# A Winograd-style 3x3 convolution: the first image pair by another queue, row sums between the loads, whole images in one store

## The chip, the core and the metric

The kernel runs on one core of a Trainium2 chip. A core has a matrix engine (TensorE, in profiles PE, with its weight loads shown apart as PEld), a vector engine (DVE), a scalar engine (ACT), GpSimd (POOL) and a sync engine (SP), all started together and ordered against each other by semaphores alone. Operands lie in SBUF with 128 partitions; TensorE writes its sums to PSUM, here eight banks of 128 x 512 fp32. Sixteen DMA engines move data between HBM and SBUF. SP issues transfers that hardware turns into packets (queue q1 in the profile); GpSimd issues transfers that software turns into packets (queue q0), and in this kernel those convert fp32 to fp16 on the way.

The metric is the device time of one launch in microseconds (us), as the median of several runs.

## What is computed

```python
x: (16, 64, 64, 64) fp32; weight: (128, 64, 3, 3) fp32
x_pad = np.pad(x, ((0, 0), (0, 0), (1, 1), (1, 1)))
for b, co, ci, kh, kw:
    output[b, co] += weight[co, ci, kh, kw] * x_pad[b, ci, kh:kh+h, kw:kw+w]
```

It is a 3x3 convolution with zero padding, over 16 images of 64 channels and 64 x 64 points, into 128 channels. The input has 16.78 MB, the weights 0.29 MB, the output 33.55 MB.

## The kernel before, in words

**Tiling.** Two images of 64 channels fill the 128 partitions, so the input comes as eight pairs, each a tile `xs` of 128 x 64 x 64 in fp16. A matmul uses 64 partitions, so the two images of a pair (`b2` = 0 and 1) run on the two halves of the array. Output rows come in four blocks of 16 rows per pair (`blk`), that is 8 even rows and 8 odd rows for each image.

**Fewer matmuls by row sums.** For each pair the kernel also forms `ss`, the sums of neighbouring input rows 2j and 2j+1. A block needs three accumulation groups (`group`, lines 110 to 145): `U` applies the middle row of weights, G1, to `ss` (6 matmuls); `A` applies G21 = w2 - w1 and G0 = w0 to rows of `xs` (12 matmuls) and gives, with `U` added, the even rows; `Bt` applies G01 = w0 - w1 and G2 = w2 (12 matmuls) and gives, with `U` added, the odd rows. A block so has 30 matmuls, and the kernel 960. Scalar copies `U` from PSUM to `ut` (line 151); Vector adds `A` and `ut` (line 156) and `Bt` and `ut` (line 159) into the output tile `ot`; SP stores each block of each image with one DMA of 512 KB (line 160), 64 in all. There are 16 such tiles.

**Weights.** SP loads them as they lie, one row of 576 fp32 per output channel (line 41). Scalar and Vector cast and reorder them into `w16`, each tap twice side by side (lines 57 to 68); TensorE transposes them by nine matmuls with an identity (lines 79 to 84), which gives each tap on both halves of the partitions; lines 86 to 90 copy and subtract them from PSUM into `Wt`.

**Loads and sums.** GpSimd issues all loads of `x`, with conversion to fp16 (line 48): pair 0 in four pieces, every other pair in two of 32 rows, 18 DMAs in all. For pair 0 Vector forms `ss` in four pieces; for pairs 1 to 7 GpSimd does so in two pieces of 2 x 1024 elements a partition (line 100). The loop of lines 44 to 53 issues all loads first, and the sums stand in line 94's loop behind it. Each engine works through its own instructions in order. `tc.keep_in_program_order` fixes the place of an instruction among those of its engine; without it a planner places the instructions by program order and due times. Waits, on data as on a free buffer, are put in by the framework.

Of the kernel before, what the change touches and what calls it, by code (L numbers as in the profile page):

```python
# [8 lines left out]
F32 = mybir.dt.float32  # L9
F16 = mybir.dt.float16  # L10


@with_exitstack
def kernel(
    ctx: ExitStack,
    tc: tile.TileContext,
    x: bass.AP,
    weight: bass.AP,
    out: bass.AP,
):  # L20
    nc = tc.nc
    B, CI, H, W = x.shape
    CO = weight.shape[0]
    assert H == 64 and W == 64 and CI == 64 and CO == 128 and B % 2 == 0
    NP = B // 2
    RB = 8

    x_rows = x.rearrange("b c h w -> (b c) h w")
    out_rows = out.rearrange("b co h w -> b co h w")
    w_flat = weight.rearrange("co ci kh kw -> co (ci kh kw)")  # L30

    const = ctx.enter_context(tc.tile_pool(name="const", bufs=1))
    psum = ctx.enter_context(tc.tile_pool(name="psum", bufs=8, space=bass.MemoryType.PSUM))
    xpool = ctx.enter_context(tc.tile_pool(name="xpool", bufs=1))
    opool = ctx.enter_context(tc.tile_pool(name="opool", bufs=16))
    spool = ctx.enter_context(tc.tile_pool(name="spool", bufs=3))
    upool = ctx.enter_context(tc.tile_pool(name="upool", bufs=4))


    w_raw = const.tile([CO, CI, 9], F32)  # L40
    nc.sync.dma_start(w_raw.rearrange("p c t -> p (c t)"), w_flat)
    xs = []
    ident = const.tile([128, 128], F16)
    for p in range(NP):
        xt = xpool.tile([128, H, W], F16, tag=f"xs{p}", name="xs")
        cuts = [0, 18, 32, 48, 64] if p == 0 else [0, 32, 64]
        for lo, hi in zip(cuts[:-1], cuts[1:]):
            nc.gpsimd.dma_start(  # L48
                xt[:, lo:hi, :], x_rows[128 * p : 128 * p + 128, lo:hi, :]
            )  # L50
            if p == 0 and lo == 0:
                make_identity(nc, ident)
        xs.append(xt)


    w16 = const.tile([CO, 9, 2, CI], F16)
    for kh in range(3):
        src = (
            w_raw[:, :, 3 * kh : 3 * kh + 3]
            .rearrange("p c t -> p t c")  # L60
            .unsqueeze(2)
            .to_broadcast([CO, 3, 2, CI])
        )
        dst = w16[:, 3 * kh : 3 * kh + 3, :, :]
        if kh == 1:
            nc.vector.tensor_copy(dst, src)  # L66
        else:
            nc.scalar.copy(dst, src)  # L68

    Wt = const.tile([128, 5, 3, CO], F16)  # L70
    G0, G21, G1, G01, G2 = range(5)

    def wrow(i):
        return Wt[:, i, :, :].rearrange("p t c -> p (t c)")

    wps = {}
    for kh in (1, 0, 2):
        wp = psum.tile([128, 512], F32, tag="acc", name="wp")
        for k in range(3):
            nc.tensor.matmul(  # L80
                wp[:, k * CO : k * CO + CO],
                w16[:, 3 * kh + k, :, :].rearrange("p d c -> p (d c)"),
                ident,
            )
        wps[kh] = wp[:, 0 : 3 * CO]
    nc.vector.tensor_copy(wrow(G1), wps[1])  # L86
    nc.scalar.copy(wrow(G0), wps[0])  # L87
    nc.vector.tensor_sub(wrow(G21), wps[2], wrow(G1))  # L88
    nc.vector.tensor_sub(wrow(G01), wps[0], wrow(G1))  # L89
    nc.scalar.copy(wrow(G2), wps[2])  # L90


    ss = []
    for p in range(NP):
        st = spool.tile([128, H // 2, W], F16, tag="ss", name="ss")
        v = xs[p].rearrange("p (j i) c -> p j i c", i=2)
        step = 8 if p == 0 else 16
        for lo in range(0, H // 2, step):
            eng = nc.vector if p == 0 else nc.gpsimd
            add = eng.tensor_add(  # L100
                st[:, lo : lo + step, :], v[:, lo : lo + step, 0, :], v[:, lo : lo + step, 1, :]
            )
            if p > 0:
                tc.keep_in_program_order(add)
        ss.append(st)

        for blk in range(4):
            j0 = blk * RB

            def group(wi_rows):  # L110

                tiles = [
                    psum.tile([128, RB, W], F32, tag="acc", name="acc") for _ in range(2)
                ]
                n = 3 * len(wi_rows)
                i = 0
                for wi, off in wi_rows:
                    for kw in (1, 0, 2):
                        c_lo, c_hi = max(0, 1 - kw), min(W, W + 1 - kw)
                        for b2 in range(2):  # L120
                            p0 = 64 * b2
                            lo, hi = j0, j0 + RB
                            if off is None:
                                rhs = ss[p][p0 : p0 + 64, lo:hi, c_lo + kw - 1 : c_hi + kw - 1]
                            else:
                                while 2 * lo + off < 0:
                                    lo += 1
                                while 2 * (hi - 1) + off > H - 1:
                                    hi -= 1
                                first = 2 * lo + off  # L130
                                last = 2 * (hi - 1) + off
                                rhs = xs[p][
                                    p0 : p0 + 64,
                                    first : last + 1 : 2,
                                    c_lo + kw - 1 : c_hi + kw - 1,
                                ]
                            nc.tensor.matmul(  # L137
                                tiles[b2][:, lo - j0 : hi - j0, c_lo:c_hi],
                                Wt[p0 : p0 + 64, wi, kw, :],
                                rhs,  # L140
                                start=i == 0,
                                stop=i == n - 1,
                            )
                        i += 1
                return tiles

            U = group([(G1, None)])
            us = []
            for b2 in range(2):
                ut = upool.tile([128, RB, W], F32, tag="ut", name="ut")  # L150
                nc.scalar.copy(ut, U[b2])  # L151
                us.append(ut)
            ots = [opool.tile([128, RB, 2, W], F32, tag="ot", name="ot") for _ in range(2)]
            A = group([(G21, 1), (G0, -1)])
            for b2 in range(2):
                nc.vector.tensor_add(ots[b2][:, :, 0, :], A[b2], us[b2])  # L156
            Bt = group([(G01, 0), (G2, 2)])
            for b2 in range(2):
                nc.vector.tensor_add(ots[b2][:, :, 1, :], Bt[b2], us[b2])  # L159
                nc.sync.dma_start(  # L160
                    out_rows[2 * p + b2, :, blk * 16 : blk * 16 + 16, :],
                    ots[b2].rearrange("p j i c -> p (j i) c"),
                )


# [28 lines left out]
```

## Time and profile before

| | |
|---|---|
| median of 8 runs | 133.12 us (132.27 to 134.37) |
| the profiled execution | 133.49 us |
| its span on the core | 131.7 us |
| PE busy | 108.9 us, 83% of the span |
| DVE busy | 84.5 us, 64% |
| POOL busy | 39.6 us, 30% |
| ACT busy | 38.2 us, 29% |
| HBM read and written | 17.07 MB and 33.55 MB |
| store queue q1 | 9360 packets, 33.85 MB |
| load queue q0 | 2592 packets, 8.39 MB (counted as fp16) |

The span is what the engines and queues cover on the core; the execution's own time is 1.8 us longer. A busy share is an average over the whole span, so it doesn't say which engine is waited for at a given moment. The page also draws the span as 40 slices of 3.3 us; each digit is the busy share in tenths, and PEclk is the clock that TensorE was granted:

```profile
PE   0408999700999999999999999999999999999910
...
POOL 6823111117999283009201910290000000000000
PEclk9999999985569999999999999999999999999998
DMA  4899999999999999999999999999999999888884
GB/s 102 112 178 215 214 215 276 275 276 276 277 279 272 285 272 279 276 328 412 419 418 419 413 417 421 418 417 416 418 418 412 421 391 372 348 342 336 330 331 178
```

TensorE has a hole in the ninth and tenth slice (26 to 33 us). The DMA row is nearly full to the end. The last row counts a converting load at its fp16 size.

### The profile page before, as it was taken

The page shows a single profiled execution, that of the slowest core. Times are in us where ns is not written, and L with a number is a line of the kernel's source. Part 1 is how long each engine was busy: PE and PEld are TensorE (multiplying, and loading weights), DVE is VectorE, ACT ScalarE, POOL GpSimd, SP SyncE. Part 2 cuts the span into 40 slices and gives each one's busy share as a digit, 9 for nine tenths or more (in the row PEclk, how much of TensorE's full clock was granted, in tenths as well). Part 3 has the DMA queues.
Part 4 walks back from the last instruction along what each step waited for, and adds up shares of the span by engine and source line. Part 5 has one row for each costly group of instructions (what it writes and reads, how often), then busy time and mean ns, then how long its engine had stood idle before and what let it go on. Part 6 is the DMA issues. An engine that isn't in the chain of part 4 may idle for free.

```text
span 131.7 us, 2482 instructions
## 1 busy us (share of the span) xinstructions
PE 108.9 (83%) x969; PEld 54.1 (41%) x969; DVE 84.5 (64%) x136; ACT 38.2 (29%) x69; POOL 39.6 (30%) x38
## 2 busy tenths in 40 slices
PE   0408999700999999999999999999999999999910
PEld 0203444200345555555555555555555555555500
DVE  0226577710047778777877777777777777877750
ACT  3604033300303333333333333333333333333300
POOL 6823111117999283009201910290000000000000
PEclk9999999985569999999999999999999999999998
DMA  4899999999999999999999999999999999888884
GB/s 102 112 178 215 214 215 276 275 276 276 277 279 272 285 272 279 276 328 412 419 418 419 413 417 421 418 417 416 418 418 412 421 391 372 348 342 336 330 331 178
DMA packets 11963, 42.39 MB, mean 322 GB/s; under 512 B 1328, under 2 KB 1456, under 8 KB 11952
## 3 DMA queue, kind: packets, MB, share of 16 engines
q1 hardware_dynamic: 9360, 33.85, 64.4%
q0 software_dynamic: 2592, 8.39, 33.0%
q8 instruction: 7, 0.11, 0.3%
q14 instruction: 4, 0.03, 0.1%
HBM read 17.07 MB, written 33.55 MB: 384 GB/s over the span
## 4 chain that ended last, share of the span: by engine, by line
PE 67%; DMA 21%; issue 4%; POOL 2%; DVE 1%; ACTq 1%; DVEq 0%; ACT 0%; POOLq 0%
PE acc L137 67%; DMA xs<-in_x_dram 21%; POOL ss L100 2%; ACTq L189 1%; DVE ot L156 1%; POOL xs L48 0%; DVEq L189 0%; DVE ot L159 0%; POOL ident masks.py:197 0%; ACT ut L151 0%; POOLq L178 0%
## 5 line engine op out<-in xcount | busy, mean ns | idle before, releaser
L137 PE MATMUL acc<-xs,Wt 64*128 64x504 f16 (+3 forms) x768 | 90.9, 384 | 0.0
L137 PEld LDWEIGHTS <-Wt 64*128 64x128 f16 x960 | 53.3, 97 | 66.4 <-issue 13.5
L156 DVE TENSOR_TENSOR ot<-acc,ut 128x512 f32<-128x512 f32 x64 | 41.2, 686 | 33.0 <-PE acc L137 16.6
L151 ACT COPY ut<-acc 128x512 f32<-128x512 f32 x64 | 34.4, 589 | 78.5 <-issue 74.6
L159 DVE TENSOR_TENSOR ot<-acc,ut 128x512 f32<-128x512 f32 x64 | 41.2, 685 | 1.0 <-PE acc L137 1.0
L100 POOL TENSOR_TENSOR ss<-xs 128x1024 f16<-128x1024 f16 x14 | 29.3, 2125 | 28.7 <-issue 28.7
L137 PE MATMUL acc<-ss,Wt 64*128 64x504 f16 (+1 forms) x192 | 27.6, 392 | 12.3 <-POOL ss L100 7.8
L48 POOL DMA_DIRECT2D xs<-in_x_dram x18 | 9.7, 548 | 20.4 <-DMA xs<-in_x_dram 19.6
L80 PE MATMUL wp<-ident,w 128*128 128x128 f16 x9 | 1.3, 307 | 4.4 <-DVE w L66 4.4
L100 DVE TENSOR_TENSOR ss<-xs 128x512 f16<-128x512 f16 x4 | 1.7, 422 | 4.8 <-DMA xs<-in_x_dram 4.8
L66 DVE CAST w<-w_raw 128x384 f16<-128x384 f32 x1 | 0.8, 834 | 3.5 <-DMA w_raw<-in_weight_dram 3.5
L80 PEld LDWEIGHTS <-w 128*128 128x128 f16 x9 | 0.8, 133 | 4.7 <-DVE w L66 4.4
L68 ACT CAST w<-w_raw 128x384 f16<-128x384 f32 x2 | 1.7, 876 | 1.5 <-DMA w_raw<-in_weight_dram 1.5
L90 ACT CAST Wt<-wp 128x384 f16<-128x384 f32 x1 | 0.5, 478 | 5.1 <-DVE Wt L88 5.1
L68 ACT ACT_TABLE_LOAD x1 | 1.3, 1283 | 0.7 <-PEq L178 0.7
L88 DVE TENSOR_TENSOR Wt<-wp,Wt 128x384 f16<-128x384 f32 x1 | 0.6, 558 | 0.1
L86 DVE CAST Wt<-wp 128x384 f16<-128x384 f32 x1 | 0.5, 549 | 0.0
L89 DVE TENSOR_TENSOR Wt<-wp,Wt 128x384 f16<-128x384 f32 x1 | 0.5, 548 | 0.0
L87 ACT CAST Wt<-wp 128x384 f16<-128x384 f32 x1 | 0.5, 478 | 0.1
masks.py:199 POOL TENSOR_SCALAR_AFFINE_SELECT ident<-ident 128x128 f16<-128x128 f16 x1 | 0.3, 307 | 0.1
masks.py:197 POOL MEMSET ident<- 128x128 f16 x1 | 0.2, 224 | 0.0
L178 POOL MEMSET const-float32-0.0<- 128x1 f32 x1 | 0.1, 100 | 0.2 <-issue 0.2
(3 smaller groups left out, 0.3 us busy)
## 6 DMA issues: line engine op xcount, KB each, us to landing
out_dram<-ot SPq DMA_DIRECT2D x64, 512.0 KB, 9.9
xs<-in_x_dram POOLq DMA_DIRECT2D x14, 512.0 KB, 24.3
xs<-in_x_dram POOLq DMA_DIRECT2D x2, 256.0 KB, 8.1
w_raw<-in_weight_dram SPq DMA_DIRECT2D x1, 288.0 KB, 2.8
xs<-in_x_dram POOLq DMA_DIRECT2D x1, 288.0 KB, 7.0
xs<-in_x_dram POOLq DMA_DIRECT2D x1, 224.0 KB, 7.2
```

Source lines behind the costliest of these rows:

```text
L48: nc.gpsimd.dma_start(xt[:, lo:hi, :], x_rows[128 * p : 128 * p + 128, lo:hi, :])
L66: nc.vector.tensor_copy(dst, src)
L68: nc.scalar.copy(dst, src)
L80: nc.tensor.matmul(wp[:, k * CO : k * CO + CO], w16[:, 3 * kh + k, :, :].rearrange("p d c -> p (d c)"), ident,)
L86: nc.vector.tensor_copy(wrow(G1), wps[1])
L88: nc.vector.tensor_sub(wrow(G21), wps[2], wrow(G1))
L100: add = eng.tensor_add(st[:, lo : lo + step, :], v[:, lo : lo + step, 0, :], v[:, lo : lo + step, 1, :])
L137: nc.tensor.matmul(tiles[b2][:, lo - j0 : hi - j0, c_lo:c_hi], Wt[p0 : p0 + 64, wi, kw, :], rhs, start=i == 0, stop=i == n - 1,)
L151: nc.scalar.copy(ut, U[b2])
L156: nc.vector.tensor_add(ots[b2][:, :, 0, :], A[b2], us[b2])
L159: nc.vector.tensor_add(ots[b2][:, :, 1, :], Bt[b2], us[b2])
L189: with _tile.TileContext(nc) as tc:
```

## The change

The change has three parts.

*Pair 0 and the weights.* Pair 0 is no longer loaded by GpSimd with conversion. SP loads it as fp32 into `x0`, which takes one slot of the output tiles, in four pieces right behind the weights. Scalar casts the pieces into `xs[0]`, and Vector forms pair 0's row sums from the fp32 tile. The weights are cast by one GpSimd instruction without reordering; TensorE then reads every ninth element of `w16` and needs two matmuls of 64 columns for each tap, one for each half of the partitions. The first copy, of G1, moves from Vector to Scalar, and the order of the following work on Scalar and Vector is fixed.

*Loads and sums.* Every other pair is loaded by one DMA. GpSimd's order becomes: weight cast, loads of pairs 1 to 4, sums of pair 1, sums of pair 2, load 5, sums of pair 3, load 6, sums of pair 4, load 7, and then the sums of pairs 5, 6 and 7. The `xs` tiles have five slots in place of eight.

*Stores.* `ot` holds a whole image, 16 KB per partition, in eight slots. Each image is stored by one DMA after its last block; only the last pair's images are stored in two halves.

```diff
-    xpool = ctx.enter_context(tc.tile_pool(name="xpool", bufs=1))
-    opool = ctx.enter_context(tc.tile_pool(name="opool", bufs=16))
+    xpool = ctx.enter_context(tc.tile_pool(name="xpool", bufs=5))
+    opool = ctx.enter_context(tc.tile_pool(name="opool", bufs=8))
...
+    w_raw = const.tile([CO, CI * 9], F32)
+    nc.sync.dma_start(w_raw, w_flat)
+    x0 = opool.tile([128, H, W], F32, tag="ot", name="x0")
+    cuts = [(0, 18), (18, 34), (34, 50), (50, 64)]
+    for lo, hi in cuts:
+        nc.sync.dma_start(x0[:, lo:hi, :], x_rows[0:128, lo:hi, :])
     ident = const.tile([128, 128], F16)
...
+    make_identity(nc, ident)
+    w16 = const.tile([CO, CI * 9], F16)
+    keep(nc.gpsimd.tensor_copy(w16, w_raw))
+
+    xs = {0: xpool.tile([128, H, W], F16, tag="xs", name="xs")}
+
+    def load(p):
+        xs[p] = xpool.tile([128, H, W], F16, tag="xs", name="xs")
+        keep(nc.gpsimd.dma_start(xs[p], x_rows[128 * p : 128 * p + 128, :, :]))
+
+    for p in range(1, 5):
+        load(p)
...
+    def sums(eng, p, src, lo, n):
+        if p not in ss:
+            ss[p] = spool.tile([128, H // 2, W], F16, tag="ss", name="ss")
+        v = src.rearrange("p (j i) c -> p j i c", i=2)
+        keep(
+            eng.tensor_add(
+                ss[p][:, lo : lo + n, :], v[:, lo : lo + n, 0, :], v[:, lo : lo + n, 1, :]
+            )
         )
...
-    for kh in (1, 0, 2):
+    for kh in (1, 2, 0):
         wp = psum.tile([128, 512], F32, tag="acc", name="wp")
         for k in range(3):
...
+            t = 3 * kh + k
+            for q in (0, 64):
+                nc.tensor.matmul(wp[q : q + 64, k * CO : k * CO + CO], w16[:, t::9], ident)
         wps[kh] = wp[:, 0 : 3 * CO]
...
+    keep(nc.scalar.copy(wrow(G1), wps[1]))
+    sums(nc.vector, 0, x0, 0, RB)
+    keep(nc.vector.tensor_sub(wrow(G21), wps[2], wrow(G1)))
+    keep(nc.vector.tensor_sub(wrow(G01), wps[0], wrow(G1)))
+    for n, (lo, hi) in enumerate(cuts):
+        keep(nc.scalar.copy(xs[0][:, lo:hi, :], x0[:, lo:hi, :]))
+        if n == 0:
+            keep(nc.scalar.copy(wrow(G0), wps[0]))
+            keep(nc.scalar.copy(wrow(G2), wps[2]))
+        if n < 3:
+            sums(nc.vector, 0, x0, RB * (n + 1), RB)
...
     for p in range(NP):
...
+        if p + 1 < NP:
+            for lo in (0, 16):
+                sums(nc.gpsimd, p + 1, xs[p + 1], lo, 16)
+        if p > 0 and p + 4 < NP:
+            load(p + 4)
+        ots = [
+            opool.tile([128, H // 2, 2, W], F32, tag="ot", name="ot") for _ in range(2)
+        ]
...
-                nc.scalar.copy(ut, U[b2])
+                keep(nc.scalar.copy(ut, U[b2]))
...
-                nc.sync.dma_start(
-                    out_rows[2 * p + b2, :, blk * 16 : blk * 16 + 16, :],
-                    ots[b2].rearrange("p j i c -> p (j i) c"),
-                )
+                nc.vector.tensor_add(ots[b2][:, j0 : j0 + RB, 1, :], Bt[b2], us[b2])
+            parts = {3: (0, 64)} if p < NP - 1 else {1: (0, 32), 3: (32, 64)}
+            if blk in parts:
+                lo, hi = parts[blk]
+                for b2 in range(2):
+                    nc.sync.dma_start(
+                        out_rows[2 * p + b2, :, lo:hi, :],
+                        ots[b2].rearrange("p j i c -> p (j i) c")[:, lo:hi, :],
+                    )
```

## The prediction, made before the changed kernel was run

> **What bounds the kernel now.** I read the chain of waits first. Its columns are start, length and what; pieces are left out between these:
>
> ```profile
> 2.07 7.24 DMA xs<-in_x_dram
> ...
> 9.59 20.64 DMA xs<-in_x_dram
> ...
> 31.06 2.13 POOL ss L100
> ...
> 33.23 87.84 PE acc L137 x797
> ```
>
> Up to 31 us the end is set by loads, then by one row sum on GpSimd, then TensorE alone. The list of waits (total us, times, longest) says how loads come to hold TensorE up:
>
> ```profile
> POOL xs L48 <- DMA xs<-in_x_dram: 19.6, 10, 3.2
> ...
> PE acc L137 <- POOL ss L100: 7.8, 1, 7.8
> ```
>
> GpSimd has all 18 load issues ahead of its first sum. Each of the last ten waits until an older load has landed, the last is issued at 30.5 us, and only then comes pair 1's sum, although pair 1's two loads landed about 14.7 to 17.2 us (the issues that waited for loads 5 and 6). TensorE stands still for 7.8 us. The table by stage (us, then busy time of PE, PEld, DVE, ACT, POOL, granted clock, DMA share, GB/s) shows the second price:
>
> ```profile
> 26.00:31.00 5.00, 0.00 (x0) 0.00 (x0) 0.79 (x2) 0.00 (x0) 1.01 (x2) 0.74 1.06 280
> 31.00:36.00 5.00, 2.77 (x14) 1.19 (x15) 0.00 (x0) 1.07 (x2) 4.98 (x4) 0.50 1.04 276
> ```
>
> After the pause the clock is 0.50. The timeline gives the length of a block by the starts of its first group:
>
> ```profile
> 15.61 0.81 PE L137 MATMUL acc<-ss,Wt 64*128 64x512 f16 x6
> ...
> 18.85 0.81 PE L137 MATMUL acc<-ss,Wt 64*128 64x512 f16 x6
> ```
>
> A block is 3.24 us; the one from 33.23 to 39.02 took 5.79, so the slow clock costs 2.55. The first block, 10.28 to 15.61, likewise lost 2.1. Pairs 1 to 7 run from 33.23 to 125.66: 92.43 less 2.55, over 7, is 12.84 us a pair. Check: 10.28 + 8 x 12.84 + 7.8 + 2.55 + 2.1 = 125.5, as the trace has it. Vector's last add ends 1.4 later at 127.0, the last store's data at 130.0, the span at 131.7.
>
> The transfers are almost as full. The DMA view, stretch 60 to 100 us (packets, MB, share of 16 engines), then 30 to 50 us:
>
> ```profile
> q1 hardware_dynamic: 4561, 16.61, 102.1%
> q8 instruction: 3, 0.05, 0.4%
> ...
> q0 software_dynamic: 760, 2.77, 68.4%
> q1 hardware_dynamic: 757, 2.76, 36.5%
> ```
>
> Stores alone move 16.61 MB in 40 us, 415 GB/s (417 with all queues). Casting loads are counted at fp16 size; in fp32 they read twice that, 2 x 215 = 430 GB/s when alone (10 to 16 us). So a second bound lies close: 33.55 MB stored, 16.78 MB read, 0.29 of weights.
>
> **Startup, part by part.** The weights land at 3.55 as before. GpSimd then casts them, 128x576 fp32 to fp16, for which no row exists: below it is the identity's 128-element select (0.31 us), above it the two-input sum (2.125 us for 1024, so 1.2 for 576). I take 1.0, as the sum's row is nearer in length: ready at 4.55. It replaces three casts (0.83 to 0.88, two engines), which had the first third ready at 4.4. The nine weight matmuls become 18 of half width. Nine took 1.3 us and a weight load 133 ns; 18 x 0.13 = 2.4 if half width saves nothing, 1.3 if it saves half; a strided read of the weights could make it more. I take 2.4, six of them by 5.4. Scalar's copy of G1 (0.48) ends at 5.95, Vector's G21 and G01 (0.56, 0.55) by 7.4. Vector's first fp32 sum costs between the fp16 row (0.42) and the fp32 add from PSUM (0.69); it starts when chunk 0 of x0 lands, about 4.6, and is hidden by the G1 copy either way. TensorE's first group thus starts at **6.1** against 10.28.
>
> Moved into Scalar's order, ahead of its first ut copy, are four casts of x0. Copies of 384 and 512 elements take 478 and 589 ns, 0.87 ns an element, so the casts take 1.15, 1.03, 1.03 and 0.92. With G0 and G2 between, the third ends at 10.1. The fourth waits for chunk 3, and behind it wait ut, then the PSUM banks, then TensorE, which gets through three groups of block 0 and the first of block 1 (to about 13, on the slow clock) before it needs a bank.
>
> When does chunk 3 land? The store queue moved its first weight data about 1.9; 0.29 MB and 2.1 MB of x0 at about 415 GB/s end at 7.6, landing by 8.2, if nothing interferes. But GpSimd's load of pair 1 is issued at 4.55, and a first software packet came about 1.5 us after its issue: 6.05. From then the two queues alternate packet by packet: 760 against 757 above, each software packet taking twice its partner's time. A pair's whole 16 KB row as one packet would take 0.64 us (double today's 0.32), an x0 packet 0.16 to 0.17. Some 9 packets an engine remain: 9 x 0.81 = 7.3, landing 0.6 later, at **14.0**. Ends: 8.2 and 14.0 (16 with a quick weight cast). I take 14.0, since the alternation is in the trace. Then cast 3 ends at 14.9, ut at 15.5, the blocked group starts at 15.5; two groups (2.4) and two blocks (6.4) end pair 0 at **24.3**, where before it ended at 25.4.
>
> Here a rule speaks against the change: the Trainium skill, SBUF — State Buffer, section Who interferes with whom, says that a Vector instruction with two SBUF inputs contends with a GpSimd one that reads SBUF. Vector's x0 sums are such; in the trace they never meet GpSimd's sums. By the rule Vector's last x0 sum, near 14, may wait out a sum of pair 1 (2.1 us), with the first evictions behind it; by the rows it costs nothing. Since ut is not ready until 15.5, the rule costs at most 0.8, which I leave to the range.
>
> **Sums between loads.** Pair 1 lands near 13.5; its two sums (4.25) are done by 18, before 24.3. The 7.8 us and 2.55 us disappear. GpSimd's queue is next held by load 5, which waits for pair 0's tile (24.3), with pair 3's sums behind it; load 6 waits for pair 1 (37), load 7 for pair 2 (50), with pair 5's sums behind that: done by 55, needed at 88. Each later sum has over 20 us of cover. TensorE's pairs then end 12.84 apart: pair 6 at 101.3, pair 7 at 114.2.
>
> **Whole-image stores.** The 64 stores of 512 KB become 18: 14 of 2 MB, 4 of 1 MB. The Trainium skill, DMA: Bandwidth & Descriptors, section Rules for kernel authors, asks for at least 1 MiB per transfer; its fit, 2.0 us plus bytes at 436 GB/s, would make 64 x 3.2 = 205 us of the old stores and about 113 of the new, an estimate. The row denies the difference: queued 512 KB stores already run at 415 to 417 GB/s, so at most 4% is left to gain. I take 425 for what follows. The price is delay: nothing of a pair leaves before its last block. Eight slots of ot let pair 4 wait for pair 0's stores, gone some 20 us before. SP's issues fall from 64 to 18, hidden as before.
>
> **The sum.** Transfers without a gap: start 1.9; weights and x0 5.7; the other 48.2 MB at 425, 113.4; end 1.6 after the data as now: 122.6. TensorE's side: pair 6's first store is issued 0.65 before Vector's end (101.3 + 1.4 - 0.65 = 102.1). By then the earlier 39.8 MB are done (1.9 + 5.7 + 93.6 = 101.2), so the queue is empty, and pairs 6 and 7 remain: 102.1 + 1.3 (a lone 512 KB store takes 2.6 to land, half of it transfer) + 8.39 MB at 425 (19.7) + 1.6 = **124.7** span. Pair 7's second half, ready at 115.6, is queued in time. Around the span lie 133.49 - 131.7 = 1.8: 126.5 beside the profiled 133.49, and as that run is 0.4 above the median, **126.1** beside 133.12.
>
> **Rivals.** (1) Chunk 3 is hardly disturbed: pair 0 ends near 21 (6.1 + 12.84 + 2.1), TensorE is ahead, and the transfers alone set the end: 122.6 + 1.4 = 124.0. For it: the weight cast may be long. Against it: the alternation. (2) The startup is dearer: strided weight loads, chunk 3 at 16, then a TensorE pause that brings back the 0.50 clock (2.55). With 2 to 5 us more, pair 0 ends at 26 to 29, giving 128 to 131. For it: Scalar's and Vector's fixed orders stand behind one DMA. (3) Slower: 16 KB packets move slower in the 16 engines. The only 16 KB packets traced are the instruction queue's: 0.4% of 640 engine-us over 3 is 0.85 us each, 19 GB/s an engine against 25 for stores (16.61 MB in 1.021 x 640). At that rate 50.6 MB take 165 us, and the time would be about 170; it decides against the change below 393 GB/s, where 1.9 + 50.6/0.393 + 1.6 reaches 132.3. Against it: those packets shared their engine, and larger packets have been quicker so far (the weights' 2304-byte rows: 0.29 MB in 38.9% of 40 engine-us, 19 GB/s). (4) The first part doesn't do what it says: x0 and weights all go on SP's one queue, so two hardware queues never work together. That costs nothing by itself.
>
> **Chances and range.** Forecast 50%, rival 1 25%, rival 2 14%, rival 3 8%, something unlisted that ends near the old time 3%. Rivals 1 and 2 are faster, too. The low end, 122.0, takes 434 GB/s in the gapless sum; the high end, 130.5, most of rival 2. Under 0.5% can't be told from no change here; faster 0.87, same 0.04, slower 0.09.
>
> **What would show it.** Right: no TensorE pause at pair 1, first group near 6, fourth x0 cast near 14, DMA share near 1 to about 101, then full again from 103, two 1 MB stores last. Wrong: x0 landing by 9 (rival 1), clock 0.50 after 15 us (rival 2), store packets over 0.65 us (rival 3). A wait of TensorE for GpSimd after 25 us would overturn the middle part.

## The result, and the profile after

| | before | changed |
|---|---|---|
| median | 132.96 us (32 runs) | 129.91 us (11 runs, 127.78 to 136.1) |
| ratio | | 0.968, 95% interval 0.964 to 0.973 |
| span of the profiled execution | 131.7 us | 128.8 us |
| the same kernel in a later session | | 128.61 us (6 runs), ratio 0.960, interval 0.954 to 0.966, span 127.1 us |

The ratio leaves out executions over 1.5% above their kernel's fastest, so it is lower than the quotient of the medians; the first profiled execution is one of these, so what follows rests on the trace of the later session, and the first is shown only beside it. The change is faster by about 3 to 4%. The forecast was 5.3% (126.1 beside 133.12): right in direction, and too far by some 2 to 3 us.

The chain of waits of the changed kernel (later session; start, length, what) leads from one piece of `x0` to an unbroken run of TensorE:

```profile
2.59 11.51 DMA x<-in_x_dram
...
14.12 0.94 ACT xs L94
15.05 0.98 ACT ut L154 x2
...
16.08 99.08 PE acc L140 x882
```

GpSimd's sums have left the chain. In their place stands what the prediction priced: the last piece of `x0` lands at 14.1, Scalar casts it (0.94), copies `ut`, and only then TensorE has a PSUM bank. The chain stops at Vector's last add, at 117.7; the last 9.4 us of the span are stores. What the chain can't show is the clock behind TensorE's run. Here are the wait and the stages (us, busy time of PE, PEld, DVE, ACT, POOL, granted clock, DMA share, GB/s) in the same trace:

```profile
PE acc L140 <- ACT ut L154: 3.3, 1, 3.3
```

```profile
13.00:16.20 3.20, 0.50 (x3) 0.20 (x4) 1.32 (x3) 2.08 (x4) 1.47 (x1) 1.00 1.01 210
16.20:19.00 2.80, 2.80 (x18) 1.25 (x16) 2.80 (x6) 0.80 (x2) 2.74 (x2) 0.58 1.07 222
19.00:22.50 3.50, 3.50 (x30) 1.73 (x28) 1.69 (x4) 1.07 (x2) 2.91 (x2) 0.85 0.99 208
```

After a pause of 3.3 us the clock is 0.58, then 0.85: 18 matmuls in 2.8 us where full speed, 96 in 10, makes 27. In the first session the pause was 2.7 us and the slow stage twice as long:

```profile
16.20:19.00 2.80, 2.80 (x13) 1.03 (x14) 2.42 (x4) 1.36 (x3) 2.80 (x2) 0.50 1.02 214
19.00:22.50 3.50, 3.50 (x20) 1.40 (x18) 2.24 (x4) 0.00 (x0) 3.35 (x3) 0.52 1.02 213
```

In the timeline the last matmuls of pair 0 give way to pair 1's first group at 28.4 us in the first session and at 26.7 in the later one, against 24.3 forecast. The difference of 1.7 us between the two is also that of their spans. How a late pair 0 reaches the end shows in two later stages of the later session:

```profile
102.00:104.00 2.00, 2.00 (x22) 1.05 (x20) 1.55 (x3) 0.20 (x1) 0.00 (x0) 1.00 0.42 172
104.00:105.00 1.00, 1.00 (x12) 0.56 (x10) 0.93 (x2) 0.71 (x2) 0.00 (x0) 1.00 0.04 16
```

TensorE is busy throughout, but the DMA share is 0.42 and 0.04: everything older is stored, and pair 6 isn't finished yet. From there pairs 6 and 7 set the end, as the prediction had it, only later.

The store queue from 70 to 100 us of the later session (packets, MB, share of 16 engines), with longer rows than before:

```profile
q1 hardware_dynamic: 883, 12.89, 100.9%
```

That is 12.89 MB in 30 us, 430 GB/s, where the kernel before had 415.

### The profile page after: what moved, and what is told of

The parts are those of the page before. It is cut to its first block, busy times and chain, and to the rows that moved or that the text cites. A ratio compares the mean times of both kernels' runs of the same rounds, so it can differ in the third digit from the quotient of the medians.

```text
span 128.8 us, 2408 instructions
## 1 busy us (share of the span) xinstructions
PE 110.0 (85%) x978; PEld 54.0 (42%) x978; DVE 83.8 (65%) x134; ACT 40.8 (32%) x72; POOL 35.1 (27%) x28
## 4 chain that ended last, share of the span: by engine, by line
PE 78%; DMA 9%; SPq 1%; DVE 1%; ACT 1%; issue 1%; DVEq 0%
PE acc L140 78%; DMA x<-in_x_dram 9%; SPq L46 1%; ACT xs L94 1%; DVE ot L158 1%; DVEq L195 0%; DVE ot L161 0%; ACT ut L154 0%; SPq L42 0%; DVEq L158 0%
## 5 line engine op out<-in xcount | busy, mean ns | idle before, releaser
L140 PE MATMUL acc<-xs,Wt 64*128 64x504 f16 (+3 forms) x768 | 98.0, 387 | 2.7 <-ACT ut L154 2.7
L69 POOL TENSOR_TENSOR ss<-xs 128x1024 f16<-128x1024 f16 x14 | 29.8, 2146 | 22.3 <-PE acc L140 13.7
L140 PE MATMUL acc<-ss,Wt 64*128 64x504 f16 (+1 forms) x192 | 33.2, 389 | 1.2 <-DVE ss L69 1.2
L69 DVE TENSOR_TENSOR ss<-x 128x512 f16<-128x512 f32 x4 | 2.8, 689 | 11.8 <-DMA x<-in_x_dram 11.8
L56 POOL DMA_DIRECT2D xs<-in_x_dram x7 | 4.0, 577 | 21.4 <-PE acc L140 21.4
L94 ACT CAST xs<-x 128x1024 f16<-128x1024 f32 (+2 forms) x4 | 4.1, 1051 | 4.8 <-DMA x<-in_x_dram 4.8
L87 PE MATMUL wp<-ident,w 128*64 128x128 f16 x18 | 1.3, 328 | 4.3 <-POOL w L50 4.3
L87 PEld LDWEIGHTS <-w 128*64 128x64 f16 x18 | 1.1, 210 | 4.3 <-POOL w L50 4.3
L89 ACT CAST Wt<-wp 128x384 f16<-128x384 f32 x1 | 0.5, 478 | 3.0 <-PE wp L87 3.0
L50 POOL CAST w<-w_raw 128x576 f16<-128x576 f32 x1 | 0.7, 664 | 2.3 <-DMA w_raw<-in_weight_dram 2.3
L96 ACT CAST Wt<-wp 128x384 f16<-128x384 f32 x1 | 0.5, 478 | 0.5 <-DVE Wt L92 0.5
L97 ACT CAST Wt<-wp 128x384 f16<-128x384 f32 x1 | 0.5, 485 | 0.0
## 6 DMA issues: line engine op xcount, KB each, us to landing
out_dram<-ot SPq DMA_DIRECT2D x14, 2048.0 KB, 14.7
x<-in_x_dram SPq DMA_DIRECT2D x1, 448.0 KB, 12.1
```

Of the source, the lines that this page charges most:

```text
L50: keep(nc.gpsimd.tensor_copy(w16, w_raw))
L56: keep(nc.gpsimd.dma_start(xs[p], x_rows[128 * p : 128 * p + 128, :, :]))
L69: eng.tensor_add(ss[p][:, lo : lo + n, :], v[:, lo : lo + n, 0, :], v[:, lo : lo + n, 1, :])
L87: nc.tensor.matmul(wp[q : q + 64, k * CO : k * CO + CO], w16[:, t::9], ident)
L89: keep(nc.scalar.copy(wrow(G1), wps[1]))
L94: keep(nc.scalar.copy(xs[0][:, lo:hi, :], x0[:, lo:hi, :]))
```

## The experiments

My theory after the result: the transfers have become the bound nearly throughout, and what is still lost is lost at the start, where the late piece of `x0` makes TensorE pause and run on a slow clock, which opens gaps in the transfers. The rivals: the transfers set the end in any case and the pause costs nothing; and, for the gain itself, that one part of the change alone makes it. This table has the parts of the change and their ratios to the kernel before:

| kernel | ratio | interval | median us |
|---|---|---|---|
| sums between loads alone | 0.996 | 0.993 to 0.999 | 132.98 |
| whole-image stores alone | 1.008 | 1.005 to 1.012 | 134.17 |
| both, without the first part | 0.968 | 0.964 to 0.971 | 128.78 |
| first part and sums, stores by block | 0.995 | 0.992 to 0.998 | 132.59 |
| the whole change | 0.968 | 0.964 to 0.973 | 129.91 |
| the whole change, later session | 0.960 | 0.954 to 0.966 | 128.61 |
| the change, last cast later | 0.957 | 0.951 to 0.962 | 127.34 |

**The last cast later.** Scalar's cast and Vector's sum of the last piece go behind block 1; block 3 is the first to need them.

```diff
-    for n, (lo, hi) in enumerate(cuts):
+    for n, (lo, hi) in enumerate(cuts[:3]):
...
-        if n < 3:
+        if n < 2:
...
+            if p == 0 and blk == 1:
+                keep(nc.scalar.copy(xs[0][:, 50:64, :], x0[:, 50:64, :]))
+                sums(nc.vector, 0, x0, 3 * RB, RB)
```

> The changed kernel with two instructions moved: Scalar's cast and Vector's row sum of the last piece of x0 stand behind block 1's work in their engines' orders, where they stood ahead of the first ut copy. No transfer is touched. Theory A (Scalar's order behind one late transfer makes the TensorE pause of 2.7 us at 13.4 us, and the pause brings the 0.50 clock): the piece still lands near 14 to 15 us, but TensorE no longer pauses before block 3, the clock stays 1.00 from about 12 us, pair 0 ends near 22.2 us in place of 28.9, and the transfers become the bound: span 123 to 124.5, about 125 to 126.3 us beside 128.7. Rival B (the transfers, not TensorE, already set the end): the pause goes and the time stays within 1 us of the changed kernel.

127.34 us (127.27 to 128.31). The chain's run of TensorE now begins with its first group and has no hole:

```profile
7.09 103.39 PE acc L140 x948
```

The stage from 10 to 15 us, and the end:

```profile
10.00:15.00 5.00, 5.00 (x44) 2.46 (x42) 3.26 (x6) 2.80 (x5) 0.00 (x0) 1.00 1.02 220
...
120.00:122.00 2.00, 0.00 (x0) 0.00 (x0) 0.00 (x0) 0.00 (x0) 0.00 (x0) 0.50 0.89 377
122.00:124.00 2.00, 0.00 (x0) 0.00 (x0) 0.00 (x0) 0.00 (x0) 0.00 (x0) 0.50 0.30 127
```

The piece still landed late (15.5), so nothing changed in the transfers; the clock stayed at 1.00, pair 0 ended near 21.8, about as expected, and TensorE was done at 111.7. From 102 to 106 us, where the changed kernel's transfers had their gap, they now moved 426 GB/s. The data ran on to 124: the transfers are the bound. Theory A holds for the start; its time was 1 to 2 us too short, since the bound lies at a span of 125.5 and not at 123 to 124.5. What the pause costs in time is not settled: the ratio is 1.1% below the changed kernel's of the first session and 0.3% below that of the later one, whose interval (0.954 to 0.966) overlaps. The spread did change: these six runs lie between 127.27 and 128.31, the changed kernel's between 127.19 and 136.1.

**The loads held back.** A small GpSimd copy of the last point of `x0` stands ahead of load 1.

```diff
+    hold = const.tile([128, 1], F32)
+    keep(nc.gpsimd.tensor_copy(hold, x0[:, H - 1, W - 1 : W]))
     for p in range(1, 5):
         load(p)
```

> The changed kernel with one small GpSimd copy added that reads the last point of x0, ahead of the load of pair 1, so that no software transfer runs beside x0. Theory A (the packet alternation of the two queues makes the last piece late): it lands near 8.2 us in place of 14.65, TensorE doesn't pause, pair 0 ends near 21.5 to 22.5. The first software packet then comes near 10 us, which leaves the engines about 2 us without work and delays pair 1 by about 2 us, to about 15 to 16, still hidden: span 124 to 126, about 126 to 128 us. Rival B (the last piece is late for another reason, as a slow queue or the order of pieces): it still lands after 12 us and nothing is gained.

131.45 us, ratio 0.985 (0.980 to 0.990), worse than the changed kernel that it edits (0.960 to 0.968), and 4 us worse than the kernel above. The last piece now landed in 7.4 us from its issue, near 10 us, where beside the software queue it took 12.1. So that queue does delay it, and rival B falls. But the price was larger than I put it:

```profile
8.00:10.00 2.00, 2.00 (x14) 0.80 (x11) 1.22 (x3) 2.00 (x4) 0.00 (x0) 1.00 0.44 176
10.00:12.00 2.00, 2.00 (x14) 0.88 (x12) 0.67 (x1) 2.00 (x4) 1.99 (x4) 1.00 0.00 0
```

The engines move nothing for about 3 us and start slowly again, and the end moves by 4.2 (spans 129.7 and 125.5), while TensorE runs without a pause from 7.0 to 112.0, as in the kernel above from 7.1 to 111.7. That is the clearest sign of the bound: a gap in the transfers costs at least its whole length, and a TensorE that is done over 15 us before the end gains nothing.

**Stores by block.** The changed kernel, with the store part undone:

```diff
-            parts = {3: (0, 64)} if p < NP - 1 else {1: (0, 32), 3: (32, 64)}
+            parts = {b: (16 * b, 16 * b + 16) for b in range(4)}
```

> The changed kernel with its store part undone: each block of 16 rows of an image goes out by its own DMA of 512 KB, from the same whole-image tile. Theory A (whole-image stores delay the stores and so leave the engines short of work near 26 to 33 and 104 to 108 us, and put 9.4 us between the last store's issue and the end): TensorE as in the changed kernel, no gap of the transfers in between, and 4.7 us from Vector's end to the end of the span, so a span of 124 to 125.5, about 126 to 127.3 us, faster by 1 to 2%. Rival B (the longer packets pay, 433 to 437 GB/s against 417): slower than the changed kernel by up to 3 us.

132.59 us: slower than the change by 3 to 4%, and my expectation (faster by 1 to 2%) was wrong. The gaps did vanish, and TensorE was done at 115.4, but the queued stores ran on at some 420 GB/s until 124 and thinned out until 129. To see whether rows or timing matter, the next kernel keeps the time at which data may leave.

**Short rows, same moment.** The kernel with the later cast; each whole-image store is cut into four DMAs of 512 KB with rows of 4 KB, issued where the one was.

```diff
+                    for r in range(lo, hi, 16):
                         nc.sync.dma_start(
-                            out_rows[2 * p + b2, :, lo:hi, :],
-                            ots[b2].rearrange("p j i c -> p (j i) c")[:, lo:hi, :],
+                            out_rows[2 * p + b2, :, r : r + 16, :],
+                            ots[b2].rearrange("p j i c -> p (j i) c")[:, r : r + 16, :],
                         )
```

> The kernel with the later cast, with each whole-image store cut into four DMAs of 512 KB with rows of 4 KB, all four issued where the one was, after the image's last block. When data is ready to leave is unchanged, only the length of a row and the number of transfers differ. Theory A (the length of the rows is what the store part gains: 426 to 430 GB/s against 414 to 418): about 2.5 to 3% less rate, 129.5 to 131 us beside 127.3. Rival B (the blocks' early stores lost against the loads, or stood in the way of them, and row length is worth little): within 0.7 us of 127.3.

131.57 us (ratio 0.991, 0.988 to 0.994) beside 127.34: 4.2 us lost, with the same data ready at the same time. The store queue from 70 to 100 us of this kernel, then of the one with whole images:

```profile
q1 hardware_dynamic: 3419, 12.45, 102.0%
```

```profile
q1 hardware_dynamic: 878, 12.80, 100.1%
```

12.45 against 12.80 MB is 2.8% of rate, about 2.2 us over the 80 us that the stores take. The rest is at the end:

```profile
122.00:124.00 2.00, 0.00 (x0) 0.00 (x0) 0.00 (x0) 0.00 (x0) 0.00 (x0) 0.50 0.94 385
124.00:126.00 2.00, 0.00 (x0) 0.00 (x0) 0.00 (x0) 0.00 (x0) 0.00 (x0) 0.50 0.34 137
126.00:128.00 2.00, 0.00 (x0) 0.00 (x0) 0.00 (x0) 0.00 (x0) 0.00 (x0) 0.50 0.06 27
```

A share of 0.06 is what one engine of 16 makes that works alone from 126 to 128: the engines do not finish together, and the span waits for the last. With whole images they came down within about 3 us, here within 5. Why one engine falls behind isn't shown. Nor can this run part the length of a row from the number of transfers, since both changed.

**The sums alone.** The kernel before, with nothing but the order of sums and loads changed (one DMA per half pair, as there):

```diff
+    for p in range(5):
+        load(p)
...
+    sums(0)
     for p in range(NP):
+        if p + 1 < NP:
+            sums(p + 1)
+        if p > 0 and p + 4 < NP:
+            load(p + 4)
```

> The kernel before with only the middle part of the change: the row sums of pairs 1 and 2 stand behind the loads of pair 4 in GpSimd's order, and later sums and loads alternate; loads, weights and stores as before. Theory A (the middle part alone takes away the pause of 7.8 us and the slow clock of 2.55): pair 1 starts by about 25.5, the pause is gone, TensorE ends near 115 to 116, and then the transfers, which had no gap up to 106 us, set the end at a span of 127 to 128, about 129 us: as fast as the whole change. Rival B (TensorE set the end throughout): 133.0 less 10.3, about 122.7 us.

132.98 us, 0.4% faster: the pause that looked like 10 us of loss was worth next to nothing by itself. The chain of waits:

```profile
17.32 16.41 DMA out_dram<-ot
...
33.79 28.88 DMA out_dram<-ot
...
63.53 51.05 PE acc L149 x461
```

Without its old pause TensorE makes blocks faster than they can be stored beside the loads (stores got about 138 GB/s beside loads in the kernel before: 2.76 MB from 30 to 50 us), all 16 `ot` tiles fill up, and Vector waits for a store to give one back:

```profile
DVE ot L168 <- DMA out_dram<-ot: 8.5, 4, 3.1
```

The pause has moved from 26 us to between 50 and 64 us. Afterwards the transfers have no gap up to 125, and the data end at 128.5 against 130.0 before. I had expected 129 from the transfers' bound: theory A's 3% did not come, and TensorE as the bound (rival B) is out.

The full tiles are not what sets the time, though. The kernel with stores by block has twice the room for outputs (8 tiles of 16 KB a partition, here 16 of 4 KB), and in its trace Vector never waits for a tile. Its span is 130.5, here 130.3. The kernel with short rows has that room too, and 129.7. TensorE was done at 115.4, 119.4 and 111.1 in the three: with stores of 512 KB in rows of 4 KB the transfers end near 130 us, whenever TensorE does.

**The stores alone.** The kernel before with whole-image tiles and stores, seven slots:

```diff
-    opool = ctx.enter_context(tc.tile_pool(name="opool", bufs=16))
+    opool = ctx.enter_context(tc.tile_pool(name="opool", bufs=7))
...
+            parts = {3: (0, 64)} if p < NP - 1 else {1: (0, 32), 3: (32, 64)}
```

> The kernel before with only the store part of the change: whole images by one DMA of 2 MB, the last pair in halves, seven slots for them; loads, sums and weights as before. Theory A (the store part pays only where the transfers have no gap; here TensorE still pauses at pair 1 and ends near 125.7 us, and pairs 6 and 7 leave only after 114 us): 114 + 1.3 + 19.7 + 1.6, a span of 136 to 137, about 137 to 139 us: slower than before by 3 to 4%. Rival B (longer rows pay by themselves): 130 to 132 us.

134.17 us, 0.8% slower: the sign that theory A expected, a quarter of the size. No store goes out before 24.6 us, the last load is issued at 26.2 in place of 30.5, and TensorE's pause for GpSimd falls from 7.8 to 5.1 us:

```profile
PE acc L140 <- POOL ss L100: 5.1, 1, 5.1
```

I had held the pause to be unchanged. That the missing stores make the loads faster fits, but no run tests it alone. The gaps came as thought, in the late stages:

```profile
105.00:108.00 3.00, 3.00 (x32) 1.55 (x30) 2.27 (x4) 1.07 (x2) 0.00 (x0) 1.00 0.43 180
108.00:110.00 2.00, 2.00 (x22) 1.05 (x20) 1.42 (x4) 1.07 (x2) 0.00 (x0) 1.00 0.31 131
```

**Sums and stores, without the first part.** Both of the last two together, with five slots of `xs` and eight of `ot`, and pair 0 and the weights as before:

```diff
-    xpool = ctx.enter_context(tc.tile_pool(name="xpool", bufs=1))
-    opool = ctx.enter_context(tc.tile_pool(name="opool", bufs=16))
+    xpool = ctx.enter_context(tc.tile_pool(name="xpool", bufs=5))
+    opool = ctx.enter_context(tc.tile_pool(name="opool", bufs=8))
...
```

> The change without its first part: pair 0 loaded by GpSimd in fp16 and the weights as before, loads of half pairs, with the sums between the loads, five slots of xs and whole-image stores. Theory A (sums and stores together make the gain; the first part wins about 0.6 MB of early transfers, 1.3 us, and gives it back with the pause it brings): no pause of TensorE, a span of 126 to 127.5, about 128 to 129 us, as the whole change. Rival B (the fp32 load by the hardware queue makes the gain): 131 us or more.

128.78 us, ratio 0.968 (0.964 to 0.971), no pause (TensorE from 8.16 on in one run of 103.74 us), span 127.3: as theory A had it. The two parts that gain 0.4% and lose 0.8% alone gain 3.2% together. The sums' order removes TensorE's pause, which only pays if the blocks can leave; the long rows let them leave faster, which only pays if TensorE has them ready. The first part adds nothing that these runs can tell, as it stands in the change, and about 1% once the last cast is out of the way (0.957 against 0.968, intervals apart). That 1% includes loading each pair by one DMA in place of two, which no run has alone.

**Two attempts to get under 127.** Pair 0 also in halves:

```diff
-            parts = {3: (0, 64)} if p < NP - 1 else {1: (0, 32), 3: (32, 64)}
+            parts = {3: (0, 64)} if 0 < p < NP - 1 else {1: (0, 32), 3: (32, 64)}
```

> The kernel with the later cast, with pair 0's two images stored in halves as the last pair's are. Theory (transfers are the bound, so only a gap of theirs can be won): the stage 25 to 30 us, at 381 GB/s in the kernel with the later cast, comes up to about 425, worth 0.5 us: 126.7 to 127.1 us beside 127.3. Rival (shorter rows give it back): 127.3 or up to 127.6.

127.97 us (0.962, 0.958 to 0.966): no gain; it is above even the rival's range, but its interval overlaps that of the kernel with the later cast (0.951 to 0.962). The pieces of `x0` shared by two queues:

```diff
-    for lo, hi in cuts:
-        nc.sync.dma_start(x0[:, lo:hi, :], x_rows[0:128, lo:hi, :])
+    for i, (lo, hi) in enumerate(cuts):
+        eng = nc.sync if i % 2 else nc.scalar
+        eng.dma_start(x0[:, lo:hi, :], x_rows[0:128, lo:hi, :])
```

> The kernel with the later cast, with the first and third piece of x0 issued by Scalar instead of SP, so that both hardware queues load at the start. Theory (the start of the transfers, 282 GB/s from 2 to 5 us, is short of issued work): x0's first packets come 0.4 us or more earlier, 126.6 to 127.0 us beside 127.3. Rival (the first packets are slow whoever issues them, and the transfers' bound starts at the same time): 127.3, and as Scalar's two issues stand ahead of its table load nothing else moves.

127.88 us (0.959, 0.955 to 0.962): no gain either. From 2 to 5 us the engines moved 268 GB/s, with one queue 285, and the weights, now beside `x0` and not ahead of it, took 5.0 us to land in place of 2.8.

**The change once more.**

> The changed kernel itself once more, for a second trace of its start. If the pause of 2.7 us after 13.4 us brings the slow clock by chance of timing, this execution may show the pause without the stage at 0.50; pair 0 then ends near 25 us in place of 28.9, and the two gaps of the transfers (25 to 35 and 105 to 110 us) are smaller. If the pause always brings it: 0.50 from about 15.5 us for some 7 us again. The time: 127.5 to 131 us.

128.61 us (127.19 to 132.94). The trace is the one shown in the result: the slow clock came again, but for half as long, and pair 0 ended at 26.7. So neither form of the expectation held fully. Another trace on record answers its question: the kernel with stores by block has the same start, its first store is issued only at 18 us, and TensorE waits as long, but the clock stays at 1.00:

```profile
PE acc L140 <- ACT ut L154: 3.0, 1, 3.0
```

```profile
15.00:20.00 5.00, 3.75 (x33) 1.90 (x34) 4.24 (x8) 2.63 (x6) 4.88 (x3) 1.00 1.03 215
```

Its pair 0 ended at 25.4. From the blocked group to that end it took 9.3 us, against 11.0 in the later trace of the changed kernel and 12.1 in the first. So the slow clock cost 1.7 and 2.8 us there, and such a pause brings it in some executions and not in others: pauses of 2.7 and 3.3 us did, one of 3.0 did not. What decides it isn't shown.

## Why the prediction was right, and by what it missed

*Direction and mechanism.* The pause at pair 1 went, no wait of TensorE for GpSimd came after it, and the fourth cast became the thing waited for: it ran from 14.1 to 15.1 and from 14.7 to 15.6 in the two traces, where 14.0 to 14.9 was worked out. The rate of the long stores, taken as 425 GB/s, was 427 to 430.

*The step that was priced wrong* is this: "the blocked group starts at 15.5; two groups (2.4) and two blocks (6.4) end pair 0 at 24.3". The group started at 15.6 and 16.15 in the two traces, but what followed, 8.8 us by the forecast, took 11.0 and 12.1. It was priced at full clock, at which it takes 9.3, as the stores by block show; the other 1.7 and 2.8 are the 0.50 clock, which the prediction had only in rival 2, with "a TensorE pause that brings back the 0.50 clock (2.55)", and among its signs of being wrong ("clock 0.50 after 15 us"). Pair 0 ended at 26.7 and 28.4, 2.4 and 4.1 us late, and spans of 127.1 and 128.8 stand against 124.7 forecast, which is the same 2.4 and 4.1. That this agrees to a tenth is partly luck: in the later trace pair 6's first store was issued at 104.4, its data moved about 0.8 us after that and not 1.3, and the way from there to the end took some 0.6 longer than the 21.3 priced.

So the forecast's mechanism and one half of rival 2 were both at work. The time, 128.6 to 129.9 us, is the one that rival 2 gave (128 to 131, held for 14%) and not the forecast's 126.1. Rival 2 looked for it in strided weight loads and a last piece at 16, and neither came; its remark that Scalar's fixed order stands behind one DMA did hold.

*A second term was too small.* "Transfers without a gap: 122.6" is refuted by the kernel with the later cast, which TensorE doesn't hold up and which has a span of 125.5. Its stages account for the 2.9 us: by 10 us it had moved 30, 285 and 348 GB/s in stages of 2, 3 and 5 us, with the fp16 loads counted once; with them at fp32 that is about 3.0 MB, where the sum had 3.4, so 0.9 us; from 25 to 30 us it fell some 0.5 us short; and the engines' uneven end, 377 and 127 GB/s in the last 4 us, costs about 1.6 against an end all at once. Less 0.5 for the higher rate (427 GB/s), that is 2.5 of the 2.9 us. Rival 1's case, an undisturbed start, was put at 124.0; 127.3 is the nearest that was measured.

*Smaller terms.* The weight cast on GpSimd took 0.66 us, not 1.0; 18 weight matmuls 1.31, not 2.4, so strided weights cost nothing that shows. The first group still started at 6.86, not 6.1, since piece 0 of `x0` landed at 6.1 and not at 4.6, and Vector's sum of it (0.69) was not hidden. No software packet was seen from 4 to 8 us, where 6.05 was the forecast; that the last piece landed near the forecast is so partly luck, two errors that cancel: until then the hardware queue moved 330 GB/s and not 415, and the first software packet came at 8.1.

*The two rules.* The rule of the Trainium skill, SBUF — State Buffer, section Who interferes with whom, was left to the range at 0.8 us at most. In the kernel with the later cast a Vector sum of `x0` met a GpSimd sum: 0.835 us where the others took 0.69, and GpSimd's 2.56 in place of 2.12. Each ran longer by one to four tenths where they met; neither waited the other out. In the changed kernel, where the prediction placed it, the two met only briefly, and the Vector sum took its 0.69. The rule of the skill's page DMA: Bandwidth & Descriptors, section Rules for kernel authors, for 1 MiB or more was right in direction. The page's fit, which its section Anatomy of one DMA — SWDGE (gpsimd) path gives for one DMA issued by GpSimd, says nothing of a queue kept full by SP when it is added up, 205 against 113 us: the queued stores gained 2.8% of rate, inside the 4% that the row of before had left open. What neither rule nor row showed is that this small gain would decide the result, as the transfers were the bound.

*Rivals.* The slower one, 16 KB packets at 19 GB/s an engine, fell: 12.80 MB in 100.1% of 480 engine-us is 26.6. That the first part uses one hardware queue costs nothing, as rival 4 said.

## What to carry to other kernels

When TensorE and the transfers are both nearly full, no part is worth what its own wait suggests: the pause of 10 us was worth 0.4% alone, and 4% beside the whole-image stores (1.008 against 0.968), whose rate is 3% higher. Before pricing a removed pause, add up the bytes, the start and the end of the transfers against the span. A pause that comes back elsewhere, as at the full output tiles, can be a sign of that bound and not its cause. And a cast put in a fixed order before the eviction of PSUM makes TensorE wait for that cast's transfer; moved behind the first blocks it held nothing up, since its reader comes late.

## What the runs showed of the hardware

A TensorE pause of 2.7 us in one trace and of 3.3 in another was followed by a clock of 0.50, and one of 3.0 us was not; the slow stage lasted twice as long in one execution as in the other, with the same program, and the spans differed by as much as pair 0's end. The granted clock doesn't show every slow stage: in both traces of the changed kernel it reads 1.00 at the start, where the first group of 6 matmuls takes 1.23 us and later ones 0.65. When many stores are queued with rows of 4 KB, the 16 engines end over 5 us, the last 2 us at about one engine's share; the reason stays open. And a hardware load beside a software load of rows over four times as long took 12.1 us for 448 KB, against 7.4 with the software loads held back.
